# Gates as half of one plus tanh of half, layer norm's Silu in one operation, three more rests before its mean, and one split unit fewer made by transfer

## The chip, the core and the metric

The kernel runs on one core of a Trainium2 chip. The core has five engines, each with its own queue of instructions in a fixed order: TensorE (PE) multiplies matrices, VectorE (DVE) and ScalarE (ACT) work element by element, GpSimd (POOL) does a little arithmetic and issues some transfers, and SyncE (SP) issues most transfers. Sixteen DMA engines carry the transfers. An instruction starts when the one ahead of it on its engine has been issued and the semaphores that it waits for have arrived; so a late instruction holds back everything behind it on its engine. The metric is the device time of one execution in microseconds, and the median of several.

## The reference

A trunk of two layers over 256 latent tokens and 256 context tokens, width 1024, in float32. What this case touches is the first half of each layer:

```python
h = modulate(rmsnorm(x, norm1_g[l]), sh1, sc1)
p = h @ w_in[l]                                   # conv: 1024, q/k/v: 1536, gates: 2048 columns
a, g = jnp.split(p_glu, 2, axis=-1)
u = a * jax.nn.sigmoid(g)                         # gated unit
u = dwconv1d(u, dw, dw_b)                         # 31 taps along the tokens, per channel
u = jax.nn.silu(layernorm(u, ln_g, ln_b))
y_conv = u @ w_o
y_attn = merge_heads(neighbourhood_attention(...)) @ w_na_out[l]
g_conv, g_attn = jnp.split(jax.nn.sigmoid(p_gate), 2, axis=-1)
x = x + g1 * ((g_conv * y_conv + g_attn * y_attn) @ w_out[l])
```

Then follows a gated MLP with a convolution of width 3. The shifts, scales and gains (sh1, sc1, g1 and three more per layer) are products of a condition vector with a 1024 x 6144 matrix. Layer 0 does latent and context tokens together (512 columns); layer 1 is the last, and needs only the 256 latent columns there.

## The kernel before

Channels lie on the 128 partitions and tokens along the columns. A weight matrix is cut into units of 128 x 1024 floats, eight blocks of 128 x 128. Each float32 product is made of three in a faster format: with w = whi + wlo and h = hhi + hlo, a step `mm3` (L187 to L189) adds whi·hhi, whi·hlo and wlo·hhi. A group is eight steps, 24 matmuls, and gives 128 output channels for all columns.

There are two ways to split a unit. `wunit` loads it (`raw`, SP, L165), ACT casts whi (L168) and DVE subtracts, wlo = raw - whi (L169). `wadded`, for the units in the set `ADDED`, lets ACT cast whi (L206) and write -whi into wlo (L207), and a transfer that accumulates, issued by POOL (L208), adds raw to it. Buffers `raw`, `whi` and `wlo` go round in fours, so a load waits until the unit four back has been split.

A layer's first half runs as follows on PE: units of values, of the gated unit, of queries and keys, then 16 gate groups. Beside it run generators (`side`), each of which does one piece of work when `slot()` is called: twice in a group of 512 columns, after four steps and at its end, and once in a group of 256. The generators are the taps of the convolution (DVE, L657 and L659), the attention with its softmax (L480 scores, L504 and L520 exponentials, L507 and L525 scaling, L546 transposes, L563 values), the layer norm, and in layer 0 the dot products that make the later shifts and gains (`ada_dots`, DVE, L293). The last ones read weights from `own`, four buffers of 128 x 1024 that SP fills, and two condition rows broadcast over the partitions (`sb`, SiLU on ACT, L273). Each `own` serves two dot products. Their number per `slot()` is set by `pace`: with 1.1, a generator gives an `own`'s two dot products on about every second call.

The program is recorded in the order in which these generators are advanced; a scheduling layer then fixes the order on each engine from the dependences and that recording. So one yield more in a generator moves other engines' work too.

The layer norm (`layer_norm`, L929 to L963) sums the four channel tiles (L940 to L942), yields once, lets PE sum over the channels with a matmul of ones (L945), subtracts the mean (L948), sums squares (L340, L344, PE L358), makes the reciprocal root (L366, POOL L368, PE L374), and then normalises each tile: scale (L956, DVE), sigmoid with the bias (L957, ACT), add the bias and multiply (L958, DVE), split into `sh` (L959, ACT) and `sl` (L960, DVE).

The gates: the first five of layer 0 and the first twelve of layer 1 are copied raw from PSUM by ACT (L701) while the softmax still runs, and turned into sigmoids after the last exponential (L914); the others are made at once (L704). The merge multiplies the attention branch by its gate (L983), the convolution branch by its own (L988), adds (L989), and splits the sum into the input of the next product (L990, L991). ACT holds one set of function tables at a time; a change of set is an instruction of its own in the profile (ACT_TABLE_LOAD).

Of the kernel before, what the change touches and what calls it, by code (L numbers as in the profile page):

```python
# [43 lines left out]

U_GLU0, U_V, U_IN, U_NA, U_CO, U_WO, U_UP, U_DN = 0, 2, 6, 36, 40, 44, 52, 96
NU = 118
ADDED = {*((0, U_IN + i) for i in (*range(19), 20, 22, 24, 26, 28)), *((0, u) for u in (U_NA + 1, U_NA + 3, *range(U_CO, U_CO + 4))), *((1, U_IN + i) for i in (7, 8, 9, 14, 15, 16, 17))}
T_GLU, T_Q, T_K, T_GATE = 0, 6, 10, 14

SWAP16 = [(i + 16) % 32 for i in range(32)]  # L50
# [3 lines left out]
def trunk(ctx: ExitStack, tc: tile.TileContext, xt, cvec, crow, wall, wada, params, bias_t, rope_t, out):  # L54
# [92 lines left out]
    def pr(l, off, n):  # L147
        return par[:, l * NPAR + off : l * NPAR + off + n]
# [469 lines left out]
    for l in range(DEPTH):  # L618
# [5 lines left out]
        with ExitStack() if last else start as e1a:  # L624
# [48 lines left out]
            def glu(j, pa, pg):  # L673
                while taps and taps[0][0] <= j - NU_:
                    conv_tap(*taps.pop(0))
                sg = tmp()
                act.activation(sg[:, :T], pg[:, :T], AF.Sigmoid)
                dve.tensor_tensor(
                    us[j % NU_][:, :, PAD : PAD + S],
                    pa[:, :T].rearrange("p (s t) -> p s t", s=NS),  # L680
                    sg[:, :T].rearrange("p (s t) -> p s t", s=NS), ALU.mult,
                )
                taps.extend((j, t) for t in range(TAPS))

# [10 lines left out]
            raw_gates = []  # L695

            def gate(pool_, n, raw=True):
                ps = in_group(T_GATE + n, ALL)
                g = new_gate(pool_, n)
                if raw:  # L700
                    act.copy(g, ps[:, :T])  # L701
                    raw_gates.append(g)
                else:
                    act.activation(g, ps[:, :T], AF.Sigmoid)  # L704

            with ExitStack() as e1b:
                eb = e1b.enter_context(tc.tile_pool(name=f"eb{l}", bufs=1))
# [26 lines left out]
                if l == 0:  # L734
# [55 lines left out]
                    for k in range(KD):  # L790
                        if k % 2 == 0 and k:
                            with tc.issue_after(low[0].ins), tc.issue_after(low[1].ins):
                                wv = wunit(l, U_V + k // 2, cuts=2)
                        low = modulated(0, ps if k == 0 else pb, 1, 0, k, h1, (0, 1))
                        if k == 0:
                            with tc.issue_after(low[0].ins), tc.issue_after(low[1].ins):
                                more()
                            with tc.issue_after(queue[-1].ins):
                                v_tile(pv, wv, k, range(4), parts=(0,))
                            vmm = v_tile(pv, wv, k, range(4), parts=(1,))  # L800
                        elif k == 1:
                            with tc.issue_after(low[1].ins):
                                low_part(wg, rg, cuts[1])
                        if k == 5:
                            with tc.issue_after(lastdma[0].ins):
                                sp.dma_start(par[:, DW:], params[:, DW:])
                                sp.dma_start(rope, rope_t)
                        if k + 1 < KD:
                            nxt = ada_now(k + 1, place, None if k else vmm)
                            next(nxt)  # L810
                        v_tile(pv, wv, k, range(4), parts=range(3) if k else (2,))
                        if k + 1 < KD:
                            finish(nxt)
                        glu0(2 if k else 1)
# [94 lines left out]
                while att.busy():  # L909
                    slot()  # L910
                side.remove(arun)
                with tc.issue_after(att.exp.ins):
                    for g in raw_gates:
                        act.activation(g, g, AF.Sigmoid)  # L914

            with ExitStack() as e1c:
                ec = e1c.enter_context(tc.tile_pool(name=f"ec{l}", bufs=1))
# [11 lines left out]
                def layer_norm():  # L929

                    while taps:
                        for _ in range(6 if last else 5):
                            if taps:
                                conv_tap(*taps.pop(0))
                        yield
                    pace[0] = 1.0 if last else 1.1
                    flat = [c.rearrange("p s t -> p (s t)") for c in cb]
                    sm = tp.tile([P, 512], F32, tag="ss", name=nm("ss"))
                    eng = pool if last else dve
                    eng.tensor_tensor(sm[:, :T], flat[0], flat[1], ALU.add)  # L940
                    eng.tensor_tensor(sm[:, :T], sm[:, :T], flat[2], ALU.add)
                    dve.tensor_tensor(sm[:, :T], sm[:, :T], flat[3], ALU.add)  # L942
                    yield
                    pm = psum("po")
                    pe.matmul(pm[:, :T], one.to_broadcast([P, P]), sm[:, :T], start=True, stop=True)  # L945
                    (s2,) = sum_squares(1, T)
                    for j in range(KC):
                        dve.scalar_tensor_tensor(flat[j], pm[:, :T], -1.0 / CONV, flat[j], ALU.mult, ALU.add)  # L948
                        s2.add(flat[j], j == KC - 1)
                    for _ in range(2 if last else 5):  # L950
                        yield
                    pb = yield from rstd(s2, CONV, "po", 0 if last else 2)
                    for j in range(KC):
                        sg = tmp()
                        g, b = pr(l, LNG + j, 1), pr(l, LNB + j, 1)
                        dve.scalar_tensor_tensor(flat[j], flat[j], g, pb[:, :T], ALU.mult, ALU.mult)  # L956
                        act.activation(sg[:, :T], flat[j], AF.Sigmoid, bias=b)  # L957
                        dve.scalar_tensor_tensor(flat[j], flat[j], b, sg[:, :T], ALU.add, ALU.mult)  # L958
# [7 lines left out]
                ln = layer_norm()  # L966
                add_side(ln)
                for n in range(n, 2 * KD):
                    gate(ec, n, False)


                z = h_tiles()
# [7 lines left out]
                if not last:  # L980
                    pace[0] = 0.7
                for n, pa in branch(U_NA, oh, ol):
                    dve.tensor_tensor(gates[KD + n], pa[:, :T], gates[KD + n], ALU.mult)  # L983
# [348 lines left out]
```

## Time and profile before

| | us |
|---|---|
| median of 3 runs (1118.72 to 1119.91) | 1118.74 |
| profiled execution | 1120.4 |
| its span on the core | 1118.6 |
| PE busy | 1097.3 |
| DVE busy | 897.0 |
| ACT busy | 591.1 |
| POOL busy | 45.9 |

The profiled execution took 1.8 us more than its span, and 1.7 more than the median. The mean granted clock of PE was 0.995 of full speed. In the rows that follow, a timeline shows start, duration, engine, line, operation, what it writes and reads, how many follow each other (x), and in brackets the idle time of its engine just before it with the instruction that ended it. A row of waits shows who waited for whom: total us, times, longest. A row of groups shows busy us, mean ns of one, and idle time before.

### The profile page before, as it was taken

Reading aid. Unit: us, or ns where it says so; the run is one execution under the profiler, and the core shown is the slowest. Engines: PE = TensorE matmul, PEld = TensorE weight load, DVE = VectorE, ACT = ScalarE, POOL = GpSimd, SP = SyncE. Lnnn points to the kernel's source line nnn. Section 1 sums busy time; section 2 is a strip of 40 time slices with the busy share of each in tenths; the row PEclk is TensorE's granted clock in tenths of the full one; section 3 lists DMA queues with packets and bytes.
Section 4 is the critical chain, followed back from the end, with each engine's and each line's share of the span. In section 5 each row is a group of like instructions: output and inputs, shape, how many; then the busy total and the mean of one; then the engine's idle time right before and its main releaser. Section 6 shows DMA issues by size and latency. Waiting matters only on the chain.

```text
span 1118.6 us, 18099 instructions
## 1 busy us (share of the span) xinstructions
PE 1097.3 (98%) x6900; PEld 952.0 (85%) x6900; DVE 897.0 (80%) x1634; ACT 591.1 (53%) x974; POOL 45.9 (4%) x61
## 2 busy tenths in 40 slices
PE   8999999899999999999999999999999999999997
PEld 7677777678889988888888888989889999999997
DVE  5568898889898788888888555789799888988773
ACT  4458878445333543434343223544877657666642
POOL 1011110010000000000000000000100000000000
PEclk9999999999999999999999999999999999999999
DMA  9978663967953354554557656557863574665781
GB/s 362 288 198 223 154 165 86 280 184 217 284 164 94 112 153 151 169 170 150 170 170 215 219 186 190 181 196 196 226 187 138 151 259 156 191 196 179 222 268 57
DMA packets 60806, 211.35 MB, mean 189 GB/s; under 512 B 7344, under 2 KB 7600, under 8 KB 60720
## 3 DMA queue, kind: packets, MB, share of 16 engines
q1 hardware_dynamic: 55104, 190.77, 53.1%
q0 software_dynamic: 5328, 19.40, 9.1%
q8 instruction: 54, 0.88, 0.3%
q14 instruction: 32, 0.26, 0.1%
q10 hardware_dynamic: 288, 0.04, 0.0%
HBM read 187.63 MB, written 1.05 MB: 169 GB/s over the span
## 4 chain that ended last, share of the span: by engine, by line
PE 77%; issue 7%; DVE 6%; ACT 5%; DMA 3%; SPq 1%; POOL 0%; POOLq 0%; DVEq 0%; ACTq 0%
PE main L187 23%; PE main L189 23%; PE main L188 23%; PE main L729 4%; DVE cb L659 3%; SPq L721 1%; DMA raw<-in_wall 1%; DMA sb<-in_crow 1%; PE sc L189 1%; PE sc L188 1%; DMA wlo<-raw 1%; PE sc L187 1%; ACT whi L206 1%; ACT wlo L207 1%; DVE wlo L169 1%
## 5 line engine op out<-in xcount | busy, mean ns | idle before, releaser
L187 PE MATMUL main<-h,whi 128*128 128x256 f32 (+1 forms) x1328 | 446.8, 337 | 0.0
L189 PE MATMUL main<-h,wlo 128*128 128x256 f32 (+1 forms) x1328 | 444.0, 336 | 2.6 <-DMA wlo<-raw 1.6
L188 PE MATMUL main<-h,whi 128*128 128x256 f32 (+1 forms) x1328 | 442.6, 334 | 0.1
L168 ACT CAST whi<-raw 128x1024 fp32r<-128x1024 f32 (+1 forms) x207 | 213.9, 1037 | 235.9 <-DMA raw<-in_wall 115.5
L169 DVE TENSOR_TENSOR wlo<-raw,whi 128x1024 fp32r<-128x1024 f32 (+1 forms) x207 | 248.3, 1206 | 91.2 <-ACT whi L168 90.3
L189 PEld LDWEIGHTS main<-h,wlo 128*128 128x128 f32 x1328 | 249.7, 189 | 32.1 <-DMA wlo<-raw 1.8
L187 PEld LDWEIGHTS main<-h,whi 128*128 128x128 f32 x1328 | 249.7, 188 | 30.7 <-issue 2.2
L188 PEld LDWEIGHTS main<-h,whi 128*128 128x128 f32 x1328 | 250.1, 189 | 28.4 <-DVE h L390 0.5
L659 DVE SCALAR_TENSOR_TENSOR cb<-u,par,cb 128x512 f32<-128x512 f32 (+1 forms) x240 | 144.3, 616 | 3.0
L187 PE MATMUL main<-fh,whi 128*128 128x256 f32 (+1 forms) x386 | 123.0, 319 | 0.0
L188 PE MATMUL main<-fl,whi 128*128 128x256 f32 (+1 forms) x386 | 122.9, 318 | 0.0
L189 PE MATMUL main<-fh,wlo 128*128 128x256 f32 (+1 forms) x386 | 122.9, 318 | 0.0
L293 DVE CUSTOM_DVE_ANT_0 t<-raw,sb,par 128x1024 bf16<-128x1024 f32 x72 | 91.5, 1278 | 0.0
L189 PEld LDWEIGHTS main<-fh,wlo 128*128 128x128 f32 x386 | 72.7, 188 | 5.6
L188 PEld LDWEIGHTS main<-fl,whi 128*128 128x128 f32 x386 | 72.7, 188 | 5.6
L187 PEld LDWEIGHTS main<-fh,whi 128*128 128x128 f32 x386 | 72.7, 188 | 5.5
L1059 ACT ACTIVATE t<-main,par 128x512 f32<-128x512 f32 (+1 forms) x82 | 50.7, 669 | 39.2 <-PE main L189 39.2
L206 ACT CAST whi<-raw 128x1024 fp32r<-128x1024 f32 x37 | 38.9, 1052 | 47.2 <-PE main L188 24.5
L293 DVE CUSTOM_DVE_ANT_0 t<-own,sb,par 128x1024 bf16<-128x1024 f32 x48 | 60.1, 1279 | 3.9 <-ACT g L704 3.9
L1060 DVE SCALAR_TENSOR_TENSOR t<-main,par,t 128x510 f32<-128x510 f32 (+1 forms) x82 | 47.6, 615 | 10.6 <-ACT t L1059 10.3
L1063 DVE SCALAR_TENSOR_TENSOR t<-main,par,t 128x510 f32<-128x510 f32 (+1 forms) x82 | 46.6, 610 | 0.0
L389 ACT ACTIVATE h<-t,mod 128x256 fp32r<-128x256 f32 x56 | 25.5, 502 | 37.8 <-DVE t L388 37.8
(222 smaller groups left out, 1295.1 us busy)
## 6 DMA issues: line engine op xcount, KB each, us to landing
raw<-in_wall SPq DMA_DIRECT2D x239, 512.0 KB, 4.4
raw<-in_wada SPq DMA_DIRECT2D x64, 512.0 KB, 4.5
wlo<-raw POOLq DMA_DIRECT2D x37, 512.0 KB, 6.2
own<-in_wada SPq DMA_DIRECT2D x24, 512.0 KB, 4.9
bias<-in_bias_t SPq DMA_DIRECT2D x8, 520.0 KB, 5.0
row<-in_wada SPq DMA_DIRECT2D x8, 512.0 KB, 4.8
sb<-in_crow SPq DMA_DIRECT2D x5, 512.0 KB, 5.9
x<-in_xt SPq DMA_DIRECT2D x8, 256.0 KB, 4.4
```

Of the source, the lines that this page charges most:

```text
L168: act.copy(hi[:, c], r[:, c])
L169: dve.tensor_tensor(lo[:, c], r[:, c], hi[:, c].bitcast(F32), ALU.subtract)
L187: pe.matmul(ps, w[0], xh, start=start, stop=False)
L188: pe.matmul(ps, w[0], xl, start=False, stop=False)
L189: pe.matmul(ps, w[1], xh, start=False, stop=stop)
L206: act.copy(hi, r)
L293: dve.tensor_tensor_reduce(tmp().bitcast(BF16), r, v, 1.0, pr(l, BADA + n, 1), ALU.mult, ALU.add, mods[l][:, n, s : s + 1])
L659: dve.scalar_tensor_tensor(cb[j], src, w, cb[j], ALU.mult, ALU.add)
L729: mm = pe.matmul(pv[t], h1[n == 1][k][:, c], w[n == 2][:, b], start=k + n == 0, stop=k == KD - 1 and n == 2)
L1059: act.activation(c, pv_, AF.Identity, bias=pr(l, FDB + t, 1), scale=w[1])
L1060: dve.scalar_tensor_tensor(c[:, :, 1:], pv_[:, :, : S - 1], w[0], c[:, :, 1:], ALU.mult, ALU.add)
L1063: dve.scalar_tensor_tensor(c[:, :, : S - 1], pv_[:, :, 1:], w[2], c[:, :, : S - 1], ALU.mult, ALU.add)
```

## The change

It has four parts.

1. `ADDED` loses one unit of layer 1, that of its fourth gate group (gate 3). It is split by L168 and L169 instead of L206, L207 and the transfer of POOL.
2. Sigmoids become tanh: sigmoid(x) = (1 + tanh(x/2)) / 2. The gated unit computes (tanh + 1)·a, twice its value, and the convolution's weights are halved once, by two operations on POOL after their load. All gates take tanh straight from PSUM; the raw copies and the second pass are gone. The merges compute (tanh + 1)·p, and the half comes in where the sum is split.
3. Layer norm's activation is one Silu with the bias on ACT; the operation on DVE that added the bias and multiplied is gone.
4. In layer 0 the layer norm yields four times instead of once between its sum and the matmul of the mean.

```diff
-ADDED = {..., *((1, U_IN + i) for i in (7, 8, 9, 14, 15, 16, 17))}
+ADDED = {..., *((1, U_IN + i) for i in (7, 8, 9, 14, 15, 16))}
...
-                act.activation(sg[:, :T], pg[:, :T], AF.Sigmoid)
-                dve.tensor_tensor(
+                act.activation(sg[:, :T], pg[:, :T], AF.Tanh, scale=0.5)
+                dve.scalar_tensor_tensor(
                     us[j % NU_][:, :, PAD : PAD + S],
-                    pa[:, :T].rearrange("p (s t) -> p s t", s=NS),
-                    sg[:, :T].rearrange("p (s t) -> p s t", s=NS), ALU.mult,
+                    sg[:, :T].rearrange("p (s t) -> p s t", s=NS), 1.0,
+                    pa[:, :T].rearrange("p (s t) -> p s t", s=NS), ALU.add, ALU.mult,
                 )
...
-                if raw:
-                    act.copy(g, ps[:, :T])
-                    raw_gates.append(g)
-                else:
-                    act.activation(g, ps[:, :T], AF.Sigmoid)
+                act.activation(g, ps[:, :T], AF.Tanh, scale=0.5)
...
                                 sp.dma_start(par[:, DW:], params[:, DW:])
+                                for i in range(DEPTH):
+                                    dw = pr(i, DW, KC * TAPS)
+                                    pool.tensor_scalar(dw, dw, 0.5, 0.0, ALU.mult, ALU.add)
...
-                with tc.issue_after(att.exp.ins):
-                    for g in raw_gates:
-                        act.activation(g, g, AF.Sigmoid)
...
-                    yield
+                    for _ in range(1 if last else 4):
+                        yield
                     pm = psum("po")
...
-                        act.activation(sg[:, :T], flat[j], AF.Sigmoid, bias=b)
-                        dve.scalar_tensor_tensor(flat[j], flat[j], b, sg[:, :T], ALU.add, ALU.mult)
-                        act.copy(sh_[j], flat[j])
-                        dve.tensor_tensor(sl_[j], flat[j], sh_[j].bitcast(F32), ALU.subtract)
+                        act.activation(sg[:, :T], flat[j], AF.Silu, bias=b)
+                        act.copy(sh_[j], sg[:, :T])
+                        dve.tensor_tensor(sl_[j], sg[:, :T], sh_[j].bitcast(F32), ALU.subtract)
...
-                    dve.tensor_tensor(gates[KD + n], pa[:, :T], gates[KD + n], ALU.mult)
+                    dve.scalar_tensor_tensor(gates[KD + n], gates[KD + n], 1.0, pa[:, :T], ALU.add, ALU.mult)
...
-                    dve.tensor_tensor(t, pc[:, :T], gates[n], ALU.mult)
+                    dve.scalar_tensor_tensor(t, gates[n], 1.0, pc[:, :T], ALU.add, ALU.mult)
                     dve.tensor_tensor(t, t, gates[KD + n], ALU.add)
-                    act.copy(z[0][n][:, :T], t)
-                    dve.tensor_tensor(z[1][n][:, :T], t, z[0][n][:, :T].bitcast(F32), ALU.subtract)
+                    act.mul(z[0][n][:, :T], t, 0.5)
+                    dve.scalar_tensor_tensor(z[1][n][:, :T], t, 0.5, z[0][n][:, :T].bitcast(F32), ALU.mult, ALU.subtract)
```

How the order changes at three places. In the rows, `main` is the result of a group, `po` that of the mean, `ss` the sum of the channel tiles, `cb` a channel tile of the convolution, and the number behind a name tells tiles apart. In the new program lines up to L698 and beyond are some numbers lower: L940 is the former L945, L935 and L936 the former L941 and L942, L698 the gates' activation.

PE, layer 0, around the mean of the layer norm. Before, near the end of a gate group:

```order
L188 MATMUL main_2332<-h_196,whi_2335 128x512
L189 MATMUL main_2332<-h_188,wlo_2336 128x512
L187 MATMUL main_2332<-h_189,whi_2335 128x512
L188 MATMUL main_2332<-h_197,whi_2335 128x512
L189 MATMUL main_2332<-h_189,wlo_2336 128x512
L187 MATMUL main_2332<-h_190,whi_2335 128x512
L188 MATMUL main_2332<-h_198,whi_2335 128x512
L945 MATMUL po_2313<-ss_2297,one 128x512
L189 MATMUL main_2332<-h_190,wlo_2336 128x512
L187 MATMUL main_2372<-h_183,whi_2374 128x512
L188 MATMUL main_2372<-h_191,whi_2374 128x512
```

Now, in the next group (main_2352, the former main_2372):

```order
L187 MATMUL main_2352<-h_188,whi_2354 128x512
L188 MATMUL main_2352<-h_196,whi_2354 128x512
L189 MATMUL main_2352<-h_188,wlo_2355 128x512
L940 MATMUL po_2377<-ss_2294,one 128x512
L187 MATMUL main_2352<-h_189,whi_2354 128x512
L188 MATMUL main_2352<-h_197,whi_2354 128x512
```

The mean's matmul has moved 19 matmuls later.

DVE, the same place, from the second `own` on to the last sum of the channel tiles. Before:

```order
L293 ISA t_2291,mod_108<-own_2197,sb_2162,par 128x1024
...
L659 SCALAR_TENSOR_TENSOR cb_3_202<-u_3_215,par,cb_3_202 128x512
L293 ISA t_2293,mod_108<-own_2197,sb_2165,par 128x1024
...
L659 SCALAR_TENSOR_TENSOR cb_3_202<-u_3_215,par,cb_3_202 128x512
L169 TENSOR_TENSOR wlo_2375<-raw_2373,whi_2374 128x1024
L659 SCALAR_TENSOR_TENSOR cb_3_202<-u_3_215,par,cb_3_202 128x512 x3
L169 TENSOR_TENSOR wlo_2469<-raw_2467,whi_2468 128x1024
L659 SCALAR_TENSOR_TENSOR cb_3_202<-u_3_215,par,cb_3_202 128x512 x3
L942 TENSOR_TENSOR ss_2297<-ss_2297,cb_3_202 128x512
```

Now, from the third `own` on:

```order
L293 ISA t_2332,mod_108<-own_2244,sb_2159,par 128x1024
...
L293 ISA t_2334,mod_108<-own_2244,sb_2162,par 128x1024
...
L169 TENSOR_TENSOR wlo_2355<-raw_2353,whi_2354 128x1024
...
L293 ISA t_2371,mod_108<-own_2292,sb_2159,par 128x1024
...
L293 ISA t_2373,mod_108<-own_2292,sb_2162,par 128x1024
...
L659 SCALAR_TENSOR_TENSOR cb_3_202<-u_3_215,par,cb_3_202 128x512
L169 TENSOR_TENSOR wlo_2457<-raw_2455,whi_2456 128x1024
L659 SCALAR_TENSOR_TENSOR cb_3_202<-u_3_215,par,cb_3_202 128x512
L936 TENSOR_TENSOR ss_2294<-ss_2294,cb_3_202 128x512
```

Four more dot products, those of the third and fourth `own`, now stand ahead of the sum; the taps and the splits between are as many as before, with the taps one by one.

ACT, layer 0, at the last softmax. Before:

```order
L520 ACTIVATE pp_1991,sm_357_1992<-main_1946,mx_355_1989 128x256
L914 ACT_TABLE_LOAD
L914 ACTIVATE g_0_1803<-g_0_1803 128x512
L525 ACTIVATE pp_1991<-pp_1991,ri_358_1995 128x256 x2
L701 COPY g_3_2039<-main_2001 128x512
L914 ACTIVATE g_1_1843<-g_1_1843 128x512
L914 ACTIVATE g_2_1999<-g_2_1999 128x512
L552 COPY pT_2064<-sc_2065 128x2x4x64
```

Now:

```order
L520 ACTIVATE pp_1993,sm_357_1994<-main_1948,mx_355_1991 128x256
L168 CAST whi_2271<-raw_2270 128x1024
L525 ACTIVATE pp_1993<-pp_1993,ri_358_1997 128x256 x2
L698 ACTIVATE g_3_2041<-main_2003 128x512
L552 COPY pT_2066<-sc_2067 128x2x4x64
```

The table load and the second passes are gone, and the cast of a later unit (whi_2271, before behind the L552 copies) has come in. Its subtraction on DVE (L169, the one that starts at 194.90 in the timeline of before) has moved with it, from behind the sum of the third channel tile (L941) and eight taps to one tap ahead of that sum. Over the whole program, ACT's table loads go from 16 to 6.

More of the change, by code (lines that the diff above doesn't have):

```diff
@@ L46 @@
 NU = 118
-ADDED = {*((0, U_IN + i) for i in (*range(19), 20, 22, 24, 26, 28)), *((0, u) for u in (U_NA + 1, U_NA + 3, *range(U_CO, U_CO + 4))), *((1, U_IN + i) for i in (7, 8, 9, 14, 15, 16, 17))}
+ADDED = {*((0, U_IN + i) for i in (*range(19), 20, 22, 24, 26, 28)), *((0, u) for u in (U_NA + 1, U_NA + 3, *range(U_CO, U_CO + 4))), *((1, U_IN + i) for i in (7, 8, 9, 14, 15, 16))}
 T_GLU, T_Q, T_K, T_GATE = 0, 6, 10, 14
@@ L693, in glu_groups, with gate @@
                     glu(j, pa, pg)
-            raw_gates = []
-            def gate(pool_, n, raw=True):
+            def gate(pool_, n):
                 ps = in_group(T_GATE + n, ALL)
                 g = new_gate(pool_, n)
-                if raw:
-                    act.copy(g, ps[:, :T])
-                    raw_gates.append(g)
-                else:
-                    act.activation(g, ps[:, :T], AF.Sigmoid)
+                act.activation(g, ps[:, :T], AF.Tanh, scale=0.5)
             with ExitStack() as e1b:
@@ L968, in trunk @@
                 for n in range(n, 2 * KD):
-                    gate(ec, n, False)
+                    gate(ec, n)
                 z = h_tiles()
```

## The prediction

> **What bounds the kernel now.** I read the page first (busy shares and the chain that ended last), then the waits of TensorE (PE), then the timelines around the longest of them, and last the groups by form. An execution is measured to about 0.2% (2.2 us); less counts as no change.
>
> ```profile
> PE 1097.3 (98%) x6900; PEld 952.0 (85%) x6900; DVE 897.0 (80%) x1634; ACT 591.1 (53%) x974; POOL 45.9 (4%) x61
> ...
> PE 77%; issue 7%; DVE 6%; ACT 5%; DMA 3%; SPq 1%; POOL 0%; POOLq 0%; DVEq 0%; ACTq 0%
> ```
>
> PE is busy for 98% of the span, and the change removes no matmul. So no saving on ScalarE (ACT) or VectorE (DVE) counts by itself; only a PE wait that it shortens does. These are the longest:
>
> ```profile
> PE po L945 <- DVE ss L942: 4.9, 1, 4.9
> ...
> PE main L189 <- DMA wlo<-raw: 1.6, 1, 1.6
> PE sc L480 <- ACT pT L552: 1.1, 1, 1.1
> PE main L189 <- DVE wlo L169: 1.1, 2, 0.6
> ...
> PE pt L546 <- ACT pp L525: 0.3, 1, 0.3
> ```
>
> One wait stands out: the matmul of the layer norm's mean (L945) in layer 0. Here it is on PE, and the granted clock around it (the columns are busy time and count of PE, PEld, DVE, ACT and POOL, then the clock, the DMA share and GB/s):
>
> ```profile
> 215.61 0.40 PE L189 MATMUL main<-h,wlo 128*128 128x512 f32 x1
> ...
> 217.94 0.40 PE L187 MATMUL main<-h,whi 128*128 128x512 f32 x1
> 218.18 0.40 PE L188 MATMUL main<-h,whi 128*128 128x512 f32 x1
> 223.50 2.04 PE L945 MATMUL po<-ss,one 128*128 128x512 f32 x2 [4.93 <-DVE ss L942]
> ```
>
> ```profile
> 217.41:220.82 3.41, 1.16 (x5) 0.59 (x4) 3.34 (x5) 1.04 (x1) 0.00 (x0) 1.00 0.94 298
> 220.82:224.23 3.41, 0.73 (x1) 0.50 (x2) 2.43 (x4) 0.00 (x0) 0.00 (x0) 0.51 0.76 296
> 224.23:227.65 3.42, 3.42 (x8) 2.15 (x7) 2.07 (x4) 1.64 (x3) 0.00 (x0) 0.50 0.01 2
> 227.65:231.06 3.41, 3.41 (x16) 2.77 (x15) 2.85 (x6) 1.98 (x4) 0.89 (x1) 0.99 0.55 111
> ```
>
> Ten matmuls take 2.33 us, 0.233 each, so PE was ready at 218.41 and stood 5.09 us. Then it ran from 223.50 to 227.65 at half clock, which costs another 2.07. The whole loss here is 7.1 us: the largest thing that this change can win.
>
> **The rests (term 1).** What L945 waits for is DVE's own queue:
>
> ```profile
> 194.90 1.22 DVE L169 TENSOR_TENSOR wlo<-raw,whi 128x1024 fp32r<-128x1024 f32 x1
> ...
> 200.39 4.68 DVE L659 SCALAR_TENSOR_TENSOR cb<-u,par,cb 128x512 f32<-128x512 f32 x6
> 208.98 1.29 DVE L293 CUSTOM_DVE_ANT_0 t<-own,sb,par 128x1024 bf16<-128x1024 f32 x1 [3.91 <-ACT g L704]
> ...
> 210.19 1.28 DVE L293 CUSTOM_DVE_ANT_0 t<-own,sb,par 128x1024 bf16<-128x1024 f32 x1
> ...
> 211.40 0.75 DVE L659 SCALAR_TENSOR_TENSOR cb<-u,par,cb 128x512 f32<-128x512 f32 x1
> 212.06 1.28 DVE L293 CUSTOM_DVE_ANT_0 t<-own,sb,par 128x1024 bf16<-128x1024 f32 x1
> ...
> 215.79 1.23 DVE L169 TENSOR_TENSOR wlo<-raw,whi 128x1024 fp32r<-128x1024 f32 x1
> 216.93 2.33 DVE L659 SCALAR_TENSOR_TENSOR cb<-u,par,cb 128x512 f32<-128x512 f32 x3
> ...
> 222.66 0.69 DVE L942 TENSOR_TENSOR ss<-ss,cb 128x512 f32<-128x512 f32 x1
> ```
>
> From start to start, a dot product (L293) takes 1.21, a tap (L659) 0.66, a split (L169) 1.14. Between the first dot product, at 208.98, and L942 stand 4 dot products, 9 taps and 2 splits: 4.84 + 5.94 + 2.28 = 13.1; shown are 13.7, since six of the taps stand back to back in threes, at some 0.1 more each. L942 ends at 223.35, PE starts 0.15 later.
>
> The three extra yields move L945 behind 19 more matmuls on PE, 4.43 us. But they also advance the generator of dot products, and DVE now has 8 of those ahead of L942 in place of 4; taps and splits stay 9 and 2. With T the start of the first, the mean's sum ends at T + 9.68 + 5.94 + 2.28 + 0.69 and PE starts at T + 18.7. Measured by the work that PE has done by then, before is worth 223.50 + 4.43 = 227.93. **If T stays at 208.98, PE starts at 227.7: the rests win 0.2 us**, not 4.4. The dot products moved ahead fill what the rests make free.
>
> So T decides. DVE is free at 205.07 and waits 3.91 us. The row names ACT, but the gate's L704 feeds no dot product; what the first one needs is its weights, `own`. These are in a crowd of transfers:
>
> ```profile
> 196.14 0.33 SPq L165 DMA_DIRECT2D raw<-in_wall  x1
> 196.56 0.86 SPq L271 DMA_DIRECT2D sb<-in_crow  x2
> 197.47 2.49 SPq L155 DMA_DIRECT2D own<-in_wada  x4
> ```
>
> ```profile
> DMA packets 963, 3.56 MB, mean 270 GB/s; under 512 B 96, under 2 KB 96, under 8 KB 962
> ...
> own<-in_wada SPq DMA_DIRECT2D x4, 512.0 KB, 12.5
> ...
> wlo<-raw POOLq DMA_DIRECT2D x1, 512.0 KB, 10.9
> ```
>
> The `raw` of 196.14 goes out when the split of 194.90 ends (196.12) and frees its buffer. In the new order that split stands nine taps earlier, ahead of the third channel tile's sum, since ACT's cast for it has moved ahead of the last softmax scaling; so this `raw` is issued some 7 us sooner (nine taps of 0.78, as in the row of six) and is out of the crowd. 512 KB at 270 GB/s is 1.9 us: T falls to about 207.1. Bounds: 208.98 (nothing) and 205.07 (DVE is not ready sooner). I take 207.1, as the bytes ahead are what the rows show. PE then starts at 225.8 and wins 2.1.
>
> Half clock: PE would stand about 0.5 at the next unit's split (its L169 ends at T + 11.8 = 218.9, six dot products and five taps ahead of it) and 3.2 before L945. Windows of the grid shown would be busy 85%, 53% and 54%. The rows show 34% and 21% followed by half clock and 100% by full, and nothing between. From no half clock at all to two windows, the cost is 0 to 0.9 + 1.7 = 2.6; I take the middle, 1.3, against 2.07 before: 0.8 won. Term 1 is **2.9**, between 0.2 and 6.2 (T = 205.07, full clock).
>
> [...]
>
> **Tanh for Sigmoid, Silu in one (term 2: 0).** On ACT, 10 of 16 table loads go, and the 17 second passes over raw gates:
>
> ```profile
> L677 ACT ACT_TABLE_LOAD x4 | 5.1, 1283 | 0.1
> L914 ACT ACTIVATE g<-g 128x256 f32<-128x256 f32 x12 | 4.4, 419 | 0.1
> L914 ACT ACTIVATE g<-g 128x512 f32<-128x512 f32 x5 | 3.1, 644 | 0.0
> ```
>
> That is 12.8 + 7.5 = 20.3 us of an engine busy for 53%. Where does PE wait for ACT? At L546 (0.3): the last scaling there stands behind a load and a sigmoid, 1.9 us, now behind one cast, which PE's last use of its buffer released before; that wait goes. But it lies 35 us ahead of L945, which DVE times: what is won there is waited again. At L480 (1.1), ACT's order just before (cast, negation, copies) is unchanged and starts from a DVE result that follows PE: it stays. If that cover fails, either is worth 0.3 to 1.1.
>
> **DVE's longer and fewer operations (term 3: 0.3 won).** The nearest rows are of the same shapes:
>
> ```profile
> L983 DVE TENSOR_TENSOR g<-main,g 128x512 f32<-128x512 f32 x8 | 5.5, 688 | 2.7 <-PE main L189 2.7
> L958 DVE SCALAR_TENSOR_TENSOR cb<-cb,par,t 128x512 f32<-128x512 f32 x4 | 3.0, 747 | 0.0
> ...
> L958 DVE SCALAR_TENSOR_TENSOR cb<-cb,par,t 128x256 f32<-128x256 f32 x4 | 1.8, 483 | 0.0
> ```
>
> Each operation rewritten costs 0.06 more: 56 of them (8 in the gated units, 48 in the merges), 3.4 us. L958 goes: 3.0 in layer 0, 1.8 in layer 1. In layer 0 the merges wait for PE (2.7), so 0. In layer 1 one of PE's two waits for L169 (1.1 less the longest, 0.6, is 0.5) falls among the merges: DVE comes there 1.8 us sooner by L958 and up to 1.4 later by the merges. I take 0.3, between -0.5 and 0.5. The two scalings of the convolution weights on POOL have POOL, 4% busy, to themselves long before the first tap: nothing; uncovered each would cost a POOL operation, 0.9 us by the rows below.
>
> **The low part (term 4: 0.2 won).** Layer 1:
>
> ```profile
> 805.76 0.87 POOL L208 DMA_DIRECT2D wlo<-raw  x1 [1.47 <-ACT wlo L207]
> 810.06 0.86 POOL L208 DMA_DIRECT2D wlo<-raw  x1 [3.42 <-ACT qk L869]
> ...
> 813.61 0.38 PE L189 MATMUL main<-h,wlo 128*128 128x256 f32 x1 [1.58 <-DMA wlo<-raw]
> ...
> 800.00:815.00 15.00, 13.42 (x104) 11.24 (x103) 14.86 (x46) 14.65 (x34) 2.46 (x3) 1.00 0.81 210
> ```
>
> PE's 1.58 us here is the transfer of 805.76, the unit before gate 3's. Gate 3's own, 810.06, shares the DMA engines with it for the last 3.5 us; without it the first lands sooner. Half of what a fair share of those 3.5 us could give (1.0) seems likely: 0.5, between 0 and 1.58. Against it DVE, full here (14.86 of 15), gets a split of 1.14 ahead of a softmax maximum (L501); all its later work moves by that. PE shows no wait for DVE there, so I charge 0.3 (0 to 1.1).
>
> **Sum.** 2.9 + 0 + 0.3 + 0.2 = 3.4 us. The profiled execution took 1120.4 (span 1118.6), so 1117.0 on that scale; the median of the runs lies 1.7 lower, 1118.74, and gives **1115.3**. Layer norm itself ends later by work done, as its mean comes 19 matmuls later; PE shows no wait for its output, so that is nothing, and up to 2 us if that cover were gone. On SP the next unit's weights now stand behind an `own` that waits for the sixth dot product, and their buffer comes free at T + 11.8; PE reads them 77 matmuls after the mean's, 18 us later.
>
> **Rivals.**
> - Wait gone: DVE finds `own` there at 205.07 and the clock stays up. Term 1 is 6.2: about 1112. For it: transfers on SP start earlier too. Against: the two `sb` still wait for PE's last attention matmul, and three more `own` are queued with the first.
> - Wait repeated: T stays 208.98. PE gets 0.2, and 0.4 to 2.1 from the clock, for PE would now stand twice, 2.4 at the split and 2.3 at L945. With the small terms 1 to 2 us: about 1117.2, hardly to be told from no change. For it: the eight dot products are in the order, certain. Against: the moved `raw`.
> - Slower: the accumulating transfer (`wlo<-raw`, 10.9 us to land) gets into the crowd ahead of `sb` and `own`, since ACT reaches its negation sooner without the gates' second passes. 1.9 us more instead of less: T = 210.9, PE at 229.6, 1.7 worse than 227.93, and half clock as before. With terms 3 and 4 at their lower ends about 1121. It decides from T = 209.2 on. Against: that transfer also ends sooner.
>
> **Chances.** 1115.3 (1113.6 to 1116.5): 0.45, all faster. Wait gone: 0.14, faster. Wait repeated (1116.5 to 1119): 0.25, nearly all within 0.2%. Slower (1119 to 1122): 0.16, of which 0.12 beyond 0.2%. So 0.59 faster, 0.29 the same, 0.12 slower. The range of 8 in 10 is 1112.0 to 1119.8; the likeliest case alone has 1113.6 to 1116.5.
>
> **What will show it.** Term 1: the first `own` dot product starts near 207, L940 (the former L945) waits about 3 us for L936, and few matmuls run at half clock; wrong if T stays, or if a new wait for L169 exceeds 1 us. Term 2: 6 table loads, ACT about 20 us less busy, and PE's L480 wait still there. Term 3: merges 0.75 each at 512 columns, PE's wait near 896 smaller. Term 4: the wait near 812 at about 1.1 us. A new wait above 1 us for a softmax chain after 806 would make the sum wrong.

## The result and the profile after

The kernel after takes 1113.31 us (median of 6 executions, 1111.86 to 1117.34), the kernel before 1119.59 in the same comparison: a ratio of 0.9945, with a 95% interval from 0.9935 to 0.9956. The prediction was 1115.3, range 1112.0 to 1119.8.

The busy lines of the page, and PE's waits, of after:

```profile
PE 1096.7 (99%) x6900; PEld 951.5 (86%) x6900; DVE 893.0 (80%) x1627; ACT 570.5 (51%) x946; POOL 45.6 (4%) x62
```

```profile
PE po L940 <- DVE ss L936: 3.0, 1, 3.0
PE sc L137 <- POOL ident masks.py:199: 1.8, 1, 1.8
PE main L189 <- DVE wlo L169: 1.6, 3, 0.6
...
PE pt L590 <- DVE t L604: 0.5, 1, 0.5
PE sc L480 <- ACT pT L552: 0.4, 1, 0.4
PE main L723 <- ACT h L389: 0.3, 1, 0.3
```

ACT is 20.6 us less busy, DVE 4.0. The waits for the mean's matmul (4.9 before) and for the copies of L552 (1.1) are smaller, those for L525 (0.3) and for `wlo<-raw` (1.6) are gone. The waits for L169 went from 1.1 in two places to 1.6 in three.

Where the time comes from is read by setting the start of each PE instruction in after against its counterpart in before. PE is 0.8 us ahead behind the scores at 103 us, 1.4 behind those of 136, and 2.2 at 190. The mean's matmul itself has another position; behind it, when both have done the same matmuls, the lead is 4.5. It stays at about 4.4 until layer 1, jumps to 6.1 at 813, and ends at 6.3, the difference of the spans (1118.6 and 1112.3).

DVE and PE at the mean, and the transfers, after:

```profile
186.48 1.22 DVE L169 TENSOR_TENSOR wlo<-raw,whi 128x1024 fp32r<-128x1024 f32 x1
...
205.05 1.28 DVE L293 CUSTOM_DVE_ANT_0 t<-own,sb,par 128x1024 bf16<-128x1024 f32 x1 [1.43 <-DMA own<-in_wada]
...
219.28 1.28 DVE L293 CUSTOM_DVE_ANT_0 t<-own,sb,par 128x1024 bf16<-128x1024 f32 x1
...
223.06 0.69 DVE L936 TENSOR_TENSOR ss<-ss,cb 128x512 f32<-128x512 f32 x1
```

```profile
187.72 0.33 SPq L165 DMA_DIRECT2D raw<-in_wall  x1
194.09 0.80 SPq L271 DMA_DIRECT2D sb<-in_crow  x2
194.95 2.30 SPq L155 DMA_DIRECT2D own<-in_wada  x4
```

```profile
220.49 0.40 PE L189 MATMUL main<-h,wlo 128*128 128x512 f32 x1
223.90 1.81 PE L940 MATMUL po<-ss,one 128*128 128x512 f32 x2 [3.02 <-DVE ss L936]
```

```profile
220.46:223.88 3.42, 0.42 (x2) 0.01 (x1) 3.26 (x6) 0.00 (x0) 0.00 (x0) 1.00 1.06 311
223.88:227.29 3.41, 3.39 (x7) 2.02 (x8) 1.54 (x3) 0.63 (x1) 0.00 (x0) 0.54 1.01 348
227.29:230.70 3.41, 3.41 (x16) 2.78 (x15) 2.75 (x5) 2.89 (x5) 0.00 (x0) 0.96 0.58 169
```

The row of the first dot product now names its releaser, the landing of `own`. T is 205.05, from there to PE's start are 18.85 us (18.7 predicted), and PE waits 3.0 (3.2 predicted). One window was 12% busy and is followed by one at 0.54 of the clock; in before there were two. The `raw` of the moved split goes out at 187.72, before at 196.14.

T is 3.93 us earlier than before, 2.05 more than predicted. Only 1.4 of it is a faster landing: `own` is issued at 194.95 and used 10.1 later, before at 197.47 and 11.5 later. The other 2.5 are an earlier issue. The `sb` loads wait for PE's last attention matmul, and PE reached it earlier. These are PE's last attention matmuls, first before, then after:

```profile
194.33 1.95 PE L563 MATMUL sc<-pT,V 128*64 128x256 f32 x16
```

```profile
192.07 1.95 PE L563 MATMUL sc<-pT,V 128*64 128x256 f32 x16
```

and SP's own waits between 180 and 210 us, first before, then after:

```profile
SPq L165 <- DVE wlo L169: 9.8, 1, 9.8
```

```profile
SPq L165 <- DVE wlo L169: 3.3, 1, 3.3
SPq L271 <- PE sc L563: 6.0, 1, 6.0
```

PE's last attention matmul ends at 194.02 in after and at 196.27 before, and `sb` is issued 0.1 and 0.3 us behind it. Before, something else ended at the same time: the `raw` of 196.14 stands ahead of `sb` in SP's queue and had waited 9.8 us for the split of 194.90. While it stood there, `sb` could not have gone sooner, whatever PE won. So the earlier issue needed both, PE's 2.2 us and the moved split. A run below, with nine more matmuls ahead of the attention's end, has the moved split without PE's 2.2; no run has PE's 2.2 without the moved split.

### The profile page after: what moved, and what is told of

Its sections match the earlier page's. It is cut to its first block, busy times and chain, and to the rows that moved or that the text cites. A ratio compares the mean times of both kernels' runs of the same rounds, so it can differ in the third digit from the quotient of the medians.

```text
span 1112.3 us, 18066 instructions
## 1 busy us (share of the span) xinstructions
PE 1096.7 (99%) x6900; PEld 951.5 (86%) x6900; DVE 893.0 (80%) x1627; ACT 570.5 (51%) x946; POOL 45.6 (4%) x62
## 4 chain that ended last, share of the span: by engine, by line
PE 85%; DVE 5%; DMA 4%; ACT 3%; SPq 2%; issue 1%; DVEq 0%; ACTq 0%
PE main L187 25%; PE main L189 25%; PE main L188 25%; PE main L723 4%; DMA raw<-in_wall 3%; SPq L715 1%; DVE cb L659 1%; DMA own<-in_wada 1%; PE sc L189 1%; PE sc L188 1%; PE sc L187 1%; PE po L563 1%; DVE wlo L169 1%; DVE t L293 1%; ACT whi L168 1%
## 5 line engine op out<-in xcount | busy, mean ns | idle before, releaser
L168 ACT CAST whi<-raw 128x1024 fp32r<-128x1024 f32 (+1 forms) x208 | 214.7, 1036 | 245.3 <-DMA raw<-in_wall 118.0
L169 DVE TENSOR_TENSOR wlo<-raw,whi 128x1024 fp32r<-128x1024 f32 (+1 forms) x208 | 249.2, 1205 | 91.0 <-ACT whi L168 89.9
L206 ACT CAST whi<-raw 128x1024 fp32r<-128x1024 f32 x36 | 37.8, 1051 | 53.8 <-PE main L188 35.6
```

Of the source, the lines that this page charges most:

```text
L168: act.copy(hi[:, c], r[:, c])
L169: dve.tensor_tensor(lo[:, c], r[:, c], hi[:, c].bitcast(F32), ALU.subtract)
L206: act.copy(hi, r)
```

## The experiments

My theory after the result: PE gains 2.2 us in the attention stage, by tanh; the loads behind it start sooner by that, so the gain goes through the mean's wait and is not lost there; the rests add nothing; the wait near 812 us is gone with gate 3's transfer. The rival is the prediction's own: what is won ahead of the mean is waited again. The runs were made on three occasions, each with its own runs of before (medians 1119.69, 1119.76 and 1120.24 us), so ratios are compared. A ratio is estimated from all runs of both kernels and differs here by up to 0.0008 from the quotient of the two medians.

### The rests alone, on the kernel before

```diff
-                    yield
+                    for _ in range(1 if last else 4):
+                        yield
                     pm = psum("po")
```

> The kernel before with the rests alone: four yields instead of one ahead of the mean's matmul. My theory: in the order of this kernel eight dot products (L293) stand ahead of the last channel sum (L942), and the split at 194.90 us stays where it was; so the first dot product starts at 209 as before, PE resumes at the mean's matmul near 227.7, and the time is that of before within 2 us (ratio 0.998 to 1.001). Rival, the rests work by themselves: the mean's matmul comes 4.4 us later, the wait falls to below 1 us, ratio 0.994 to 0.996.

Measured: 1121.6 us, ratio 1.0009 (0.9991 to 1.0027). From its timeline:

```profile
208.78 1.28 DVE L293 CUSTOM_DVE_ANT_0 t<-own,sb,par 128x1024 bf16<-128x1024 f32 x1 [4.34 <-ACT g L704]
...
227.64 1.10 PE L946 MATMUL po<-ss,one 128*128 128x512 f32 x2 [1.49 <-DVE ss L942]
```

PE resumes at 227.64, as the eight dot products said (227.7). The named wait fell from 4.9 to 1.5, most of the way to what the rival wanted, and yet nothing that shows was won: part of the idling stands now at the split ahead of the mean (PE waits 3.4 for L169 in four places, before 1.1 in two). A wait that shrinks is not yet a gain.

### Tanh and Silu alone

`ADDED` and the single yield as in before, the activations as in after:

```diff
-ADDED = {..., (7, 8, 9, 14, 15, 16))}
+ADDED = {..., (7, 8, 9, 14, 15, 16, 17))}
...
-                    for _ in range(1 if last else 4):
-                        yield
+                    yield
```

(against the kernel after)

> The kernel before with tanh for the sigmoids and Silu in one operation, without the rests and with gate 3 of layer 1 still split by transfer. Theory formed from the trace after: PE waits 2.2 us less in the attention stage (near 103, 136 and 189 us), and since the broadcast loads (sb) wait for PE's last attention matmul, the dot products start as much sooner and 1.4 more from less crowding, at 205.0; L936 ends at 219.4 and PE resumes at 219.6 instead of 223.5. The time is 3.9 to 4.5 us below before (ratio 0.9960 to 0.9965), and the wait of the mean's matmul is about 3.3 us. Rival, as in my prediction: what is won ahead of that matmul is waited again, and ACT's savings give 0 to 1 us.

Measured: 1113.62 us, ratio 0.9938 (0.9918 to 0.9958): the whole gain of the change.

```profile
204.39 1.28 DVE L293 CUSTOM_DVE_ANT_0 t<-own,sb,par 128x1024 bf16<-128x1024 f32 x1 [1.66 <-DMA own<-in_wada]
...
218.91 2.05 PE L939 MATMUL po<-ss,one 128*128 128x512 f32 x2 [3.49 <-DVE ss L936]
```

PE still waits 3.49 here, and resumes 4.6 us earlier than before. The rival falls. The gain is larger than the theory's 3.9 to 4.5; the interval's upper end, 0.9958, lies just below the range given.

### Everything but the rests

```diff
-                    for _ in range(1 if last else 4):
-                        yield
+                    yield
```

(against the kernel after)

> The kernel after with one yield ahead of the mean's matmul as before: everything but the rests. Theory: the same as after within 1 us (1112.3 to 1114.3), since the rests let four more dot products of 4.84 us in ahead of the sum for 4.43 us of matmuls. Rival, the rests carry the gain at that place: 4 us slower than after.

Measured: 1112.48 us, ratio 0.9937 (0.9912 to 0.9961), against 0.9945 with them: no difference that these runs show. The rests, the part with the most promise, carry nothing that the intervals, some 0.2% to either side, would show.

### The dot products held during the rests

```diff
+                    if not last:
+                        pace[0] = 0.0
                     for _ in range(1 if last else 4):
                         yield
+                    if not last:
+                        pace[0] = 1.1
                     pm = psum("po")
```

(against the kernel after)

> The kernel after, with the pace of the dot products set to 0 during the four rests, so that only four of them stand ahead of the sum, and the mean's matmul 13 matmuls later than in before. Theory: PE arrives at the mean's matmul at 219.3 and the sum is ready at 219.4, so the wait of 3.0 us and the half clock behind it (1.7 us) go: 1108 to 1110 us. Rival: the dot products held back come late for their readers or crowd DVE behind the mean, and the gain is given back: 1112 to 1115.

Measured: 1118.03 us, ratio 0.9986 (0.9972 to 0.9999). The mean's wait is 0.2, and behind it PE leads after by 4.9 us, as the theory said. All of it and more is given back some 135 us later:

```profile
335.90 1.28 DVE L293 CUSTOM_DVE_ANT_0 t<-own,sb,par 128x1024 bf16<-128x1024 f32 x1
...
342.26 1.28 DVE L293 CUSTOM_DVE_ANT_0 t<-own,sb,par 128x1024 bf16<-128x1024 f32 x1
```

```profile
354.83 0.58 PE L189 MATMUL sc<-h,wlo 128*128 128x256 f32 x1 [5.39 <-DVE wlo L169]
```

The generator has to be finished before the next norm. The work held back is run there in one go, six dot products between these two rows; norm and split come late, PE waits 5.4 us and then runs at half clock for two windows of 3.41 us (352.6 to 359.4). The lead of 4.9 becomes a lag of 3.4. The rival is right, by the first of its two reasons, and the kernel is slower than even the rival's 1112 to 1115.

### Held, and made up for in the attention branch

On top of the last one:

```diff
-                    pace[0] = 0.7
+                    pace[0] = 1.0
                 for n, pa in branch(U_NA, oh, ol):
```

> The kernel after with the dot products held during the four rests, and the pace behind layer norm, in the attention branch, at 1.0 instead of 0.7, so that none is left over for the rush at the end of layer 0's first half. Theory: the 5.4 us wait for a split near 360 us that the hold alone showed, and the half clock behind it, were the rush of six dot products in a row at 336 to 343 us; without it the gain at the mean's matmul (4.9 us against after) stays: ratio to before about 0.990 (1108 to 1109.5). Rival: the dot products moved into the branch delay DVE's merges there, a wait of 1 us or more for L169 or a merge shows, and the time is that of after (ratio 0.994).

Measured: 1110.3 us (1109.86 to 1112.0), ratio 0.9916 (0.9901 to 0.9932): the fastest of all. The wait of 5.4 is gone, so the rush was its cause. The gain is some 2 us less than the theory's 0.990. From PE's waits between 200 and 320 us:

```profile
PE main L187 <- ACT h L988: 0.9, 2, 0.5
PE main L188 <- DVE h L989: 0.6, 1, 0.6
```

Of the 4.7 that PE leads behind the mean, 2.5 are lost around these rows, 1.5 of it in the waits themselves: at the end of the merges DVE has dot products between the last sums and their splits. The clock stays full there (the two windows concerned are 79% and 75% busy), so the rest of the 2.5 is not half clock.

### Held, with the pace at 1.1

```diff
-                    pace[0] = 0.7
+                    pace[0] = 1.1
                 for n, pa in branch(U_NA, oh, ol):
```

(against the held kernel)

> As e5_hold_pace, with the pace in the attention branch at 1.1 instead of 1.0. In its order two dot products fewer stand between the last merges and their splits. Theory: the waits for the last split inputs near 310 us (L988 and L989, 1.5 us together, and some half clock behind them, 2.5 in all) go, and the time is about 2 us below e5_hold_pace: ratio 0.9895 to 0.9905. Rival: DVE is as crowded in the branch itself, and the loss moves there: ratio 0.991 to 0.993.

Measured: 1115.41 us, ratio 0.9959 (0.9947 to 0.9971). The waits for L988 and L989 are gone, and these stand in their place between 200 and 320 us:

```profile
PE main L189 <- DVE wlo L169: 1.5, 1, 1.5
PE main L187 <- DVE t L986: 1.4, 1, 1.4
```

The rival is right: DVE is as full in the branch. The loss is larger than its 0.991 to 0.993: behind these waits PE runs at half clock for two windows (305.1 to 311.9), and its lead of 5.6 over the kernel after becomes a lag of 1.4. Of the three placements of the held work that were run, 1.0 is the best.

### Nine more matmuls ahead of the attention's end, or behind it

On the kernel without the rests; `(0, 3)` in the first run, `(0, 5)` in the second:

```diff
+        for _ in range(again[0]):
+            mm3(ps[:, c], ws[0], xh[0][:, c], xl[0][:, c], True, True)
         for k in range(n):
...
+                again[0] = 3 if (l, n) == (0, 3) else 0
                 ps = in_group(T_GATE + n, ALL)
+                again[0] = 0
```

> Everything but the rests (as e3_norest), with nine more matmuls of 512 columns (2.1 us; the first step of the group computed three times more, and overwritten) in layer 0's fourth gate group, ahead of PE's last attention matmuls. The order keeps the mean's matmul at the same row, so nine useful matmuls stand behind it that stood ahead. Theory, what is won or lost ahead of the attention's end passes on, since the broadcast loads wait for PE there: the first dot product starts 2.1 us later than in e3_norest, PE resumes at the mean's matmul 2.1 later with 2.1 less done: 4.2 us slower than e3_norest, ratio 0.9974. Rival, as in my prediction, DVE and its loads set that place whatever comes ahead of it: PE resumes when it did, 2.1 us slower than e3_norest, ratio 0.9956.

> As e6_up, with the nine matmuls in the sixth gate group, behind PE's last attention matmul. Both theories: the first dot product starts where it did in e3_norest, PE resumes at the mean's matmul at the same time with 2.1 us less done: 2.1 us slower than e3_norest, ratio 0.9956. The two theories differ in the distance of e6_up to this run: 2.1 us or none.

Measured: 1117.81 us, ratio 0.9984 (0.9972 to 0.9996), and 1115.23, ratio 0.9963 (0.9946 to 0.9979). The distance is 2.6 us, where the pass-through theory has 2.1 and the rival 0; the intervals just overlap. The rows say more. First and second run:

```profile
207.52 1.28 DVE L297 CUSTOM_DVE_ANT_0 t<-own,sb,par 128x1024 bf16<-128x1024 f32 x1 [2.36 <-DMA own<-in_wada]
```

```profile
204.78 1.28 DVE L297 CUSTOM_DVE_ANT_0 t<-own,sb,par 128x1024 bf16<-128x1024 f32 x1 [1.62 <-DMA own<-in_wada]
```

`sb` is issued at 196.11 and 193.62, and the first dot product starts 11.4 and 11.2 later. So the link holds in the new order, where the `raw` goes out well ahead (189.74 and 187.25): later attention, later loads, later T, 2.5 and 2.7 us for 2.1 of matmuls. The first run also shows what the moved `raw` is worth without PE's lead: its last attention matmul ends at 196.03, as in before (196.27), and T is 207.52, 1.5 earlier than before and near the 207.1 of the prediction. PE resumed only 1.2 later (220.47 and 219.31), since the scheduling layer had put two taps fewer between in the first run; that makes the step from T to the end of the execution less clean than I meant it to be. Both traces also have a wait of 3.1 and 3.4 us for `wlo<-raw` in layer 1, though gate 3's transfer is away in both and the order there is that of the run without the rests, which has none. That put the fourth term in doubt.

### Tanh alone

Against tanh and Silu together:

```diff
-                        act.activation(sg[:, :T], flat[j], AF.Silu, bias=b)
-                        act.copy(sh_[j], sg[:, :T])
+                        act.activation(sg[:, :T], flat[j], AF.Sigmoid, bias=b)
+                        dve.scalar_tensor_tensor(flat[j], flat[j], b, sg[:, :T], ALU.add, ALU.mult)
+                        act.copy(sh_[j], flat[j])
```

> The kernel before with tanh for the sigmoids of the gated unit and the gates, and the merges that go with it; layer norm's sigmoid, its multiplication, the rests and gate 3's transfer as in before. Theory: nearly all of the gain of e2_acts, 5 to 6 us (ratio 0.994 to 0.9955), since the shorter waits near 103, 136 and 189 us and the earlier dot products come from the table loads and second passes that tanh removes. Rival: Silu in one operation carries a share of more than 2 us, and this run is at 0.996 or above.

Measured: 1112.45 us, ratio 0.9938 (0.9916 to 0.9961), the same as both together. Silu adds nothing that shows; tanh carries the change. With tanh alone both things at the `sb` loads are there already: the `raw` goes out at 186.97, and PE's last attention matmul ends at 193.26. Which of tanh's own parts does it (fewer table loads, no second passes, or the order that follows from them) was not run.

### Gate 3's transfer: away from before, back in after, and after once more

```diff
-ADDED = {..., (7, 8, 9, 14, 15, 16, 17))}
+ADDED = {..., (7, 8, 9, 14, 15, 16))}
```

> The kernel before with gate 3's unit of layer 1 split by DVE instead of by the accumulating transfer, and nothing else. Theory A, from the trace after (PE's wait of 1.58 us near 812 us was gone there): 1.5 us faster, ratio 0.9985. Theory B, from e6_up and e7_down, where the same unit was split by DVE and the wait was 3.1 and 3.4 us: that wait belongs to the rate at which the transfers of that moment run, which differs between executions, and this part is worth 0 to 0.5 us, ratio 0.9995 to 1.0005.

> The kernel after, once more. Theory A: no wait near 812 us again, as in its first trace. Theory B: a wait there of anything from 0 to 3.5 us, with the transfer of the unit ahead of gate 3's taking 5 to 10 us to land. Both: ratio 0.9935 to 0.9955.

> The kernel after with gate 3's unit of layer 1 split by the accumulating transfer again. Theory A: 1.5 us slower than e10_after_again. Theory B: within 0.5 us of it.

Measured: before without the transfer 1119.41 us, ratio 0.9994 (0.9983 to 1.0005). After, once more: 1114.15, 0.9943 (0.9924 to 0.9961). After with the transfer: 1113.45, 0.9935 (0.9919 to 0.9952). Theory A's 0.9985 still lies within the first interval, but it said that the wait is gone in the kernel after, and the second trace has it. B holds, though the last two lie 0.7 us apart where it had 0.5, a distance within their intervals: the part is worth nothing that shows. The second trace of after, its wait, and the transfer waited for (the row of DMA issues between 799 and 816 us, with the us to landing last):

```profile
808.20 0.50 PE L189 MATMUL main<-h,wlo 128*128 128x256 f32 x1 [3.06 <-DMA wlo<-raw]
```

```profile
wlo<-raw POOLq DMA_DIRECT2D x1, 512.0 KB, 8.8
```

and that of its first trace, where PE did not wait:

```profile
wlo<-raw POOLq DMA_DIRECT2D x1, 512.0 KB, 5.7
```

The same program had 3.06 us of this wait in one execution and none in the other. With the transfer the five traces have 1.6, 2.9, 0.7, 2.6 and 0; without it the nine have 0, 0, 0, 0.3, 3.1, 3.4, 2.0, 3.1 and 0. What sets the rate of these transfers from one execution to the next stays open.

## Why the prediction was right or wrong

**Direction, range and most likely case.** Faster came true, inside the range, and by 6.3 us where 3.4 were forecast. The likeliest case (1113.6 to 1116.5) missed it by 0.3. That the time fell inside the range is in part luck: 2.9 of the 3.4 was put under the rests, which carry nothing that shows, and 0 under tanh, which carries everything. The moved `raw`, which term 1 counted on, is tanh's doing as well: with the rests alone it goes out at 195.53, with tanh alone at 186.97.

**Term 1, the rests.** Right: eight dot products ahead of the sum, 18.7 us from T to PE's start, the moved `raw`, a wait of 3 us, half clock for less than before; and that the rests win next to nothing while T stays: in the run of the rests alone T is 208.78 and PE resumes at 227.64, where 227.7 was forecast and 227.93 would have been worth the same as before. The stand of 0.5 at the next unit's split did not come. The term's lower end, 0.2, was too high: with T unmoved and two windows at half, 2.6 against 2.07, its own terms give -0.3. The term was given as 2.9 and the lead behind the mean is 4.5. The step that failed is T: "T falls to about 207.1", where it fell to 205.05. The fall has two parts. The crowd gave 1.4 (1.9 forecast): the three traces with the `raw` in it need 11.5 to 11.9 us from the issue of `own` to T, the eleven without it 9.5 to 11.0. I left out that the issue itself moves, 2.5 us, with PE's arrival at the end of the attention, once the `raw` no longer stands ahead of `sb` on SP. Where the extra matmuls took PE's lead away, T was 207.52: the prediction's 207.1 is what the moved `raw` gives alone.

**Term 2, tanh.** "It lies 35 us ahead of L945, which DVE times: what is won there is waited again" is the wrong step, and the costliest: the term was 0, and tanh alone carries the whole change. I had found that `sb` waits for PE's last attention matmul, and used it against the rival "wait gone"; the same fact makes DVE's timing there follow PE, as far as the `raw` ahead of `sb` is out of the way. The wait for L480 near 136 was also said to stay, because its chain starts from a DVE result that follows PE. It fell from 1.1 to 0.4: in after, DVE has the small operation for `qk` ahead of a tap, and the first of ACT's steps there comes earlier against PE. This is read from the two timelines; no run shows it alone. The gain of 0.8 near 103 was not foreseen: DVE's first gated unit starts 1.4 us earlier (61.91 against 63.27), as a table load of 1.28 us ahead of it is gone, and its backlog of taps is that much shorter when the keys are due.

**Term 3, DVE.** Half of it was a wrong price. A merge with an immediate number costs no more than the product that it replaces:

```profile
L977 DVE SCALAR_TENSOR_TENSOR g<-g,main 128x512 f32<-128x512 f32 x8 | 5.5, 683 | 2.9 <-PE main L189 2.8
L982 DVE SCALAR_TENSOR_TENSOR t<-g,main 128x512 f32<-128x512 f32 x8 | 5.4, 681 | 2.0 <-PE main L189 2.0
L951 DVE SCALAR_TENSOR_TENSOR cb<-cb,par,po 128x512 f32<-128x512 f32 x4 | 2.7, 741 | 4.0 <-PE po L374 4.0
```

0.68 us, as the product before (0.688). I had taken L958's 0.747 for it, and L958, like L951 here, reads a number per partition. The nearer row was in the trace of before: L948, with an immediate number, took 0.684. So the 56 operations cost nothing (those at 256 columns take 0.414 to 0.419, before 0.418 to 0.425), not 3.4 us of DVE. On the time neither shows: PE's lead behind 820 us goes from 6.2 to 6.3. The sign given for it did not come: PE's wait near 896 was 0.48, in after it is 0.52 (at 889.9), and another of 0.49 stands at 914.4.

**Term 4, the low part.** Forecast 0.2. In the pair of traces it looked like 1.7, in timed runs it is 0.0006 of the time, with an interval across zero. The mechanism that I gave for it, a share of the DMA engines, is not borne out by the runs.

**The half clock.** One window at half, where I took the middle between none and two. A window that was 12% busy (0.42 us of work in 3.42) was followed by half clock, as 34% and 21% before.

The traces have the windows between that the prediction lacked. In before itself, PE's wait near 812 left the window from 811.40 to 814.81 54% busy (1.83 of 3.41 us), and the clock behind it stayed full (1.00 from 814.81 to 818.23). In the second trace of the kernel after, the mean's wait of 2.92 us fell on two windows (217.80 to 221.21 and 221.21 to 224.63), 59% and 55% busy, and no half clock followed: behind 224.1 the matmuls start 0.23 us apart. In its first trace 3.02 us of the same wait fell into one window, the one 12% busy, and the next ran at half, which cost 1.7 us. With the held work at pace 1.1 a window 51% busy (301.67 to 305.08, 1.75 us) was followed by half clock: from 306.9 to 311.6 the matmuls start 0.43 us apart. So a wait of about 3 us cost half clock in one of two traces of one program and not in the other.

**The rivals.** "Wait gone" had T (205.05) and PE's resumption (223.90, where T + 18.7 gives 223.8) right, though DVE was free at 203.6 and did wait, 1.43 us. It had the clock wrong: the one window at half, worth 1.7 us, is what parts its 6.2 from the measured 4.5. "Wait repeated" is what the rests alone did. "Slower" did not come: the accumulating transfer took 11.1 us to land in that crowd against 10.9, but did not hold back `own`.

## What to carry to other kernels

Before a saving is written off as waited for again, follow the wait's own releaser back: if the loads or operations behind it start from an instruction of the engine that gains, the gain can pass through (here PE's 2.2 us came back as an issue 2.5 us earlier), unless something else in the same queue is due at that time too (before, the `raw` that had waited 9.8 us). A generator that is advanced to let time pass advances everything else that shares its slots (here four more dot products of 1.21 us), so count what else moves; and work that is held back must be given a place where the engine has room, or it comes all at once where the program has to be finished with it (here six dot products, and a wait of 5.4 us). A wait that differs between two traces of the same program (here 0 and 3.06 us) is no evidence for a change: run the part alone.

## What the runs showed that I had not expected

- The transfer ahead of gate 3's unit took 5.7 us in one execution of the kernel after and 8.8 in another, and PE waited 0 and 3.06.
- An operation with two arithmetic steps on DVE cost 0.68 us at 128 x 512 with an immediate number and 0.741 to 0.747 with a number per partition.
- After holding the dot products, 5.4 us of waiting at one place, with two windows at half clock behind it, cost 8.3 in all (from 4.9 ahead to 3.4 behind): more than the 4.9 won at the place that the change was made for.
- The same wait for the mean's matmul was followed by a window at half clock in one execution of the kernel after (3.02 us, one window 12% busy) and by none in another (2.92 us, two windows 59% and 55% busy).
